# A two-layer trunk on one core: own weight buffers for the recurrence's gate branch and the first u projection, whose chunks go to single PSUM banks

## The chip, the cores and the metric

The kernel runs on one core of one Trainium2 chip. The metric is the device time of one execution in microseconds (us), the median of several runs. The engines are TensorE (PE, its weight loads PEld), VectorE (DVE), ScalarE (ACT), GpSimd (POOL) and SyncE (SP), which issues most DMAs.

## The reference: what is computed

Two layers over 1024 latent tokens with a prefix of 256 context tokens, width 1024. Only layer 0 matters here. Its input `h` (scaled and shifted by the adaLN modulation) is projected by `ab_w_in` to five branches of width 512:

```python
xl = depthwise_conv(p[..., :W], conv_w, conv_b)                 # branch x of the recurrence
...                                                             # gates r, i from xl; a, b; two scans
y_a = h_rec.astype(pp.dtype) * jax.nn.silu(pp[..., W:2 * W])    # gate branch
u = jax.nn.gelu(pp[..., 2 * W:3 * W])
v = jax.nn.gelu(pp[..., 3 * W:4 * W])
y_b = spatial_gating(u, v, sgu_ln_g, sgu_ln_b, sgu_w, sgu_b) * jax.nn.silu(pp[..., 4 * W:5 * W])
return jnp.concatenate([y_a, y_b], axis=-1) @ w_out
```

Layer 1 is a gated convolution beside differential attention. Modulation vectors (`silu(c) @ w_mod + b_mod`) for both layers are also computed.

## The kernel before, in words

Tokens lie on the free axis, 1280 of them in three chunks `CHUNKS` of 256, 512 and 512 (line 28). A projection gives 128 features at a time. Each float32 operand is split into a high part (rounded by a copy on ACT) and a low part (the difference, by default on POOL), and three products are added: hi x hi, lo x hi, hi x lo. With 8 steps of 128 along the input width that makes 24 matmuls for a chunk.

Weights for 128 features come by `wload` (line 143). It takes a raw tile (name `wraw`, two buffers), issues its DMA on SP, and splits it in two halves of four k-steps each: `whi` by ACT (line 138), `wlo` by POOL (line 141). `whi` and `wlo` have four buffers each in the pool `wp`, so two whole projections' worth, for all callers alike. A new `whi` has to wait until TensorE has used the old tile in its buffer for the last time.

A projection runs chunk by chunk over all k-steps (`proj3c_g`, line 167). So its first weight half is read for the last time in the middle of the last chunk, and its second half at the very end. `proj1_g` (line 180) has the same order for one chunk and any destination.

PSUM: `pj3` (line 260) gives tiles of three banks, two buffers, in turn to the projections `px`, `pg`, `pu`, `pz` and to the recurrence's gates `pgate`. `psb` (line 214) gives single banks of 512 columns, two buffers, to the modulation (`modp`, `modcp`, `gatep`) and to others later.

The recurrence handles four blocks of 128 features: `lru_x(f)` projects the x branch (conv follows on DVE), `lru_g(f)` the gate branch (line 396), `lru_rec(f)` makes four gates `pgate` by small matmuls and turns them to coefficients on ACT and DVE, `lru_scan(f)` scans. `mod_do` and `mod_c` (lines 475, 487) put a piece of modulation between them. Around the change TensorE's order is: `px` of block 3, `lru_rec(2)`, `lru_g(3)`, the first u projection `pu` (line 532, GELU per chunk into `ut0`), `lru_rec(3)`, then `pz` (weights `WZ0`) and the second `pu` (weights `WU1`).

TensorE's order is written by hand (line 55). The order of ACT, DVE, POOL and SP is set by a scheduler that simulates the program when it is built; each engine then works through its own list strictly in that order. In `lru_scan` (line 442) ACT takes a square root `tt` that needs DVE's product of line 433.

Of the kernel before, what the change touches and what calls it, by code (L numbers as in the profile page):

```python
# [11 lines left out]
F32R = mybir.dt.float32r  # L12
AF = mybir.ActivationFunctionType
# [29 lines left out]
def tile_hybrid_trunk(es: ExitStack, tc: tile.TileContext, A, out, scr=None):  # L43
    nc = tc.nc
    V, S, G, T, SY = nc.vector, nc.scalar, nc.gpsimd, nc.tensor, nc.sync

    def pool(name, space=None, **kw):
        if space is not None:
            kw["space"] = space
        return tc.tile_pool(name=name, bufs=1, reuse_waits="tile", **kw)  # L50
# [6 lines left out]
    wp = es.enter_context(pool("w"))  # L57
# [71 lines left out]
    def hs(c0, n):  # L129
        if c0 < CTX:  # L130
            return hhc[:, :, c0:c0 + n], hlc[:, :, c0:c0 + n]
        return hhl[:, :, c0 - CTX:c0 - CTX + n], hll[:, :, c0 - CTX:c0 - CTX + n]

    def split(hi, lo, src, he=None, le=None):
        he = he or S
        le = le or V
        if he is S:
            S.activation(hi, src, AF.Copy)  # L138
        else:
            he.tensor_copy(hi, src)  # L140
        le.tensor_tensor(lo, src, f32(hi), op=ALU.subtract)  # L141

    def wload(src, nk=8, le=None):
        raw = wp.tile([128, nk, 128], F32, name="wraw", tag="wraw", bufs=2)
        SY.dma_start(raw, src)
        res = []
        for h in range(nk // 4):
            hi = wp.tile([128, 4, 128], F32R, name="whi", tag="whi", bufs=4)
            lo = wp.tile([128, 4, 128], F32R, name="wlo", tag="wlo", bufs=4)
            split(hi, lo, raw[:, 4 * h:4 * h + 4], le=le or G)  # L150
            res.append((hi, lo))
        return res

    def run(gen):
        for _ in gen:
            pass
# [10 lines left out]
    def proj3c_g(ps, w):  # L167
        for c0, n in CHUNKS:
            o, (hh, hl_) = ps[:, 256 + c0:256 + c0 + n], hs(c0, n)
            for k in range(KT):  # L170
                hi, lo = w[k // 4]
                T.matmul(o, hi[:, k % 4], hh[:, k], start=k == 0, stop=False)  # L172
                T.matmul(o, hi[:, k % 4], hl_[:, k], start=False, stop=False)
                T.matmul(o, lo[:, k % 4], hh[:, k], start=False, stop=k == KT - 1)  # L174
                yield 0.68 * n / 512

    def proj3(ps, w):
        run(proj3c_g(ps, w))

    def proj1_g(o, w, c0, n):  # L180
        hh, hl_ = hs(c0, n)
        for k in range(KT):
            hi, lo = w[k // 4]
            T.matmul(o, hi[:, k % 4], hh[:, k], start=k == 0, stop=False)  # L184
            T.matmul(o, hi[:, k % 4], hl_[:, k], start=False, stop=False)  # L185
            T.matmul(o, lo[:, k % 4], hh[:, k], start=False, stop=k == KT - 1)  # L186
            yield 0.65 * n / 512

    def proj1(o, w, c0, n):
        run(proj1_g(o, w, c0, n))  # L190
# [23 lines left out]
    def psb(name="psb"):  # L214
        t = ps1.tile([128, 512], F32, name=name, tag="psb", bufs=2)
        return t
# [43 lines left out]
    def pj3(name):  # L260
        t = pj.tile([128, 1536], F32, name=name, tag="pj", bufs=2)
        return t
# [75 lines left out]
    for k in range(KT):  # L338
# [14 lines left out]
        if k + 1 < KT:  # L353
            hmod(k + 1, mb)
        next(gg)
    WX1 = wload(A["w_in0"][1], le=V)
    so_cm.__exit__(None, None, None)
    run(gx), run(gg)
# [7 lines left out]
    with pool("lrua") as lp, pool("lruc") as lc:  # L366
# [6 lines left out]
        def lru_x(f):  # L373
            if f:
                p = pj3("px")
                PROJ(proj3c_g(p, WX1 if f == 1 else wload(A["w_in0"][f])))
            else:
                p = px0
            xp = lp.tile([128, 1286], F32, name="xp", tag="xp", bufs=1)
            V.memset(xp[:, 0:2], 0.0)  # L380
            V.memset(xp[:, 258:260], 0.0)
            V.memset(xp[:, 1284:1286], 0.0)
            S.activation(xp[:, 2:258], p[:, 256:512], AF.Copy)
            for c0 in (512, 1024):
                S.activation(xp[:, c0 - 252:c0 + 260], p[:, c0:c0 + 512], AF.Copy)
            cw = P("convw")[:, 4 * f:4 * f + 4]
            xl = lt("xl", "xl", 2)
            V.tensor_scalar(xl, xp[:, 0:WC], cw[:, 0:1], P("convb")[:, f:f + 1], op0=ALU.mult, op1=ALU.add)
            for j in range(1, 4):
                V.scalar_tensor_tensor(xl, xp[:, j:j + WC], cw[:, j:j + 1], xl, op0=ALU.mult, op1=ALU.add)  # L390
            xh = lt("xh", "xh", 1, F32R)
            xo = lt("xo", "xo", 1, F32R)
            split(xh, xo, xl)
            XL[f] = (xl, xh, xo)

        def lru_g(f):
            if f:
                p = pj3("pg")
                PROJ(proj3c_g(p, wload(A["w_in0"][4 + f])))
            else:  # L400
                p = pg0
            sg = ld.tile([128, NTOK], F32, name="sg", tag="sg", bufs=2)
            S.activation(sg, p[:, 256:1536], AF.Tanh, scale=0.5)
            V.scalar_tensor_tensor(sg, sg, 1.0, p[:, 256:1536], op0=ALU.add, op1=ALU.mult)
            SG[f] = sg

        def lru_rec(f):
            (wh, wl), = wload(A["wg"][f], nk=4)
            mod_step()
            xl, xh, xo = XL[f]  # L410
            bs = []
            for d in range(2):
                i8 = 4 * d + f
                gts = []
                for g in range(2):
                    p = pj3("pgate")
                    m = 2 * d + g
                    for c0, n in ((0, 258), (258, 512), (770, 512)):
                        o = p[:, 254 + c0:254 + c0 + n]
                        T.matmul(o, wh[:, m], xh[:, c0:c0 + n], start=True, stop=False)  # L420
                        T.matmul(o, wh[:, m], xo[:, c0:c0 + n], start=False, stop=False)
                        T.matmul(o, wl[:, m], xh[:, c0:c0 + n], start=False, stop=True)
                    t = lt("gt", "gr" if g == 0 else "gx", 2)
                    S.activation(t, p[:, 254:1536], AF.Tanh, scale=0.5, bias=hb[:, 8 * g + i8:8 * g + i8 + 1])
                    gts.append(t)
                r, gi = gts
                tt = lt("tt", "tt", 2)
                S.activation(tt, r, AF.Tanh, scale=sp2[:, i8:i8 + 1], bias=sp2[:, i8:i8 + 1])
                S.activation(r, r, AF.Exp, scale=sn4[:, i8:i8 + 1], bias=sn4[:, i8:i8 + 1])
                V.scalar_tensor_tensor(gi, gi, 1.0, xl, op0=ALU.add, op1=ALU.mult)  # L430
                V.scalar_tensor_tensor(tt, r, 1.0, tt, op0=ALU.add, op1=ALU.mult)
                V.tensor_scalar(r, tt, -1.0, 1.0, op0=ALU.mult, op1=ALU.add)
                V.scalar_tensor_tensor(tt, r, 1.0, tt, op0=ALU.add, op1=ALU.mult)
                bs.append((r, gi, tt))
                mod_step()
            return bs
# [78 lines left out]
        PROJ = interleave  # L515
        mod_load()
        lru_x(0)
        lru_g(0)
        lru_x(1)
        lru_scan(0, lru_rec(0))  # L520
        lru_g(1)
        lru_x(2)
        lru_scan(1, lru_rec(1))
        lru_g(2)
        lru_x(3)
        lru_scan(2, lru_rec(2))
# [2 lines left out]
        u0 = u0_cm.__enter__()  # L529
        ut0 = u0.tile([128, NTOK], F32, name="ut0")  # L530
        zt0 = u0.tile([128, NTOK], F32, name="zt0")
        p = pj3("pu")
        proj3(p, wload(A["w_in0"][8]))
        for c0, n in CHUNKS:
            S.activation(ut0[:, c0:c0 + n], p[:, 256 + c0:256 + c0 + n], AF.Gelu_apprx_tanh)
        rec3 = lru_rec(3)
        while pend or late:
            mod_do()
# [11 lines left out]
    p = pj3("pz")  # L550
# [9 lines left out]
    with pool("sguw") as vw:  # L560
# [7 lines left out]
        p = pj3("pu")  # L568
# [48 lines left out]
        p = pj3("pz")  # L617
# [38 lines left out]
    for g in (2, 3):  # L656
        w = wload(A["w_in0"][8 + g])
# [5 lines left out]
        w = wload(A["w_in0"][12 + g])  # L663
# [110 lines left out]
    def pb(name):  # L774
        t = pbp.tile([128, 512], F32, name=name, tag="pb", bufs=2)
        return t
# [102 lines left out]
    for t in range(NT):  # L879
        p = pb("pv")  # L880
# [395 lines left out]
```

## Time and profile before

| | |
|---|---|
| median of three runs | 1142.79 us (1142.55 to 1142.98) |
| the profiled execution's own time | 1142.13 us |
| its span, first to last instruction | 1140.3 us |
| PE, PEld, DVE, ACT, POOL busy | 98%, 81%, 63%, 38%, 25% of the span |
| 72 to 205 us (the recurrence): PE busy | 130.07 of 133.00 us |
| 205 to 1130 us: PE busy | 921.16 of 925.00 us |

How to read it: a row of the timeline gives start, duration, engine, line, operation and tiles; brackets tell how long the engine was idle before, and what ended that. Matmuls are pipelined: a 512-column matmul is shown as 0.39 us long, but the next starts 0.23 us after it (0.12 us for 256 columns), so a stall of TensorE is a start-to-start distance above these. The program also ends 1.83 us later than its span says (1142.13 less 1140.3).

### The profile page before, as it was taken

How to read it: one execution, taken by the hardware profiler on the slowest of the kernel's cores; microseconds unless marked ns; L12 is line 12 of the kernel's file. 1: busy time of each engine (PE TensorE's matmuls, PEld its weight loads, DVE VectorE, ACT ScalarE, POOL GpSimd, SP SyncE). 2: the span in 40 equal slices, each digit the busy share in tenths (PEclk: the TensorE clock that was granted, in tenths of full speed). 3: DMA queues.
4: the chain of work that ended last, by engine and by line, in shares of the span. 5: the costliest groups of instructions: out<-in, count | busy, mean ns of one | idle time of the engine just before them, and what ended most of it. 6: DMA issues, size and time to landing. Idle time of an engine off the chain costs nothing.

```text
span 1140.3 us, 14964 instructions
## 1 busy us (share of the span) xinstructions
PE 1116.7 (98%) x5842; PEld 920.0 (81%) x5842; DVE 720.9 (63%) x1031; ACT 436.0 (38%) x687; POOL 284.6 (25%) x228
## 2 busy tenths in 40 slices
PE   6999999999999999999999999999999999999997
PEld 4777777888888888888788788888888888888886
DVE  6777986943412566537512876777676666738986
ACT  4463665620221243343212545444544444424210
POOL 0011112530240222258402322323421321220021
PEclk9999999999999999999999999999999999999999
DMA  9654542220241543336637243442531520127641
GB/s 368 258 178 157 185 154 105 94 97 1 86 142 54 180 152 116 120 130 208 230 93 190 91 112 78 111 118 65 143 96 40 144 91 20 48 73 240 203 148 74
DMA packets 78199, 148.08 MB, mean 130 GB/s; under 512 B 6305, under 2 KB 35873, under 8 KB 77233
## 3 DMA queue, kind: packets, MB, share of 16 engines
q1 hardware_dynamic: 71088, 128.25, 33.0%
q0 software_dynamic: 7040, 18.88, 7.3%
q8 instruction: 46, 0.75, 0.3%
q14 instruction: 25, 0.20, 0.1%
HBM read 112.49 MB, written 34.62 MB: 129 GB/s over the span
## 4 chain that ended last, share of the span: by engine, by line
PE 84%; DVE 5%; DMA 4%; issue 3%; ACT 3%; POOL 1%; SPq 0%; POOLq 0%; DVEq 0%; ACTq 0%
PE pout L683 5%; PE pout L685 5%; PE pout L684 5%; PE p L184 4%; PE p L185 4%; PE p L186 4%; PE psc L992 3%; PE pv L208 3%; PE pv L209 3%; PE pv L210 3%; PE psc L993 3%; PE atr L1015 3%; PE modp L221 2%; PE pz L172 2%; PE pz L174 2%
## 5 line engine op out<-in xcount | busy, mean ns | idle before, releaser
L141 POOL TENSOR_TENSOR wlo<-wraw,whi 128x512 fp32r<-128x512 f32 x86 | 134.3, 1565 | 427.8 <-ACT whi L138 415.6
L994 DVE TENSOR_REDUCE st<-psc 128x1 f32<-128x1280 f32 x64 | 95.1, 1486 | 39.5 <-PE psc L993 39.5
L683 PE MATMUL pout<-woh,yhi 128*128 128x512 f32 (+1 forms) x296 | 114.8, 388 | 0.3 <-DVE xres L1168 0.2
L685 PE MATMUL pout<-woh,ylo 128*128 128x512 f32 (+1 forms) x296 | 114.4, 386 | 0.0
L684 PE MATMUL pout<-wol,yhi 128*128 128x512 f32 (+1 forms) x296 | 114.1, 385 | 0.0
L996 ACT ACTIVATE e<-psc,st 128x1280 f32<-128x1280 f32 x64 | 85.2, 1331 | 71.7 <-DVE st L994 68.8
L184 PE MATMUL p<-hhl,whi 128*128 128x512 f32 x256 | 105.0, 410 | 0.0
L138 ACT ACTIVATE whi<-wraw 128x512 fp32r<-128x512 f32 x92 | 57.5, 628 | 122.8 <-PE p L185 27.2
L186 PE MATMUL p<-hhl,wlo 128*128 128x512 f32 x256 | 100.5, 393 | 0.0
L185 PE MATMUL p<-hll,whi 128*128 128x512 f32 x256 | 100.3, 392 | 0.0
L138 ACT ACTIVATE ah<-atr 128x512 fp32r<-128x512 f32 (+1 forms) x96 | 47.1, 525 | 64.6 <-PE atr L1015 64.2
L992 PE MATMUL psc<-k,qh 128*128 128x512 f32 (+1 forms) x192 | 67.1, 364 | 2.6 <-ACT e L996 2.5
L993 PE MATMUL psc<-k,ql 128*128 128x512 f32 (+1 forms) x192 | 68.7, 358 | 0.0
L683 PEld LDWEIGHTS pout<-woh,yhi 128*128 128x128 f32 x296 | 55.6, 188 | 12.4 <-issue 0.6
L685 PEld LDWEIGHTS pout<-woh,ylo 128*128 128x128 f32 x296 | 55.6, 188 | 11.6 <-DVE ylo L141 0.2
L684 PEld LDWEIGHTS pout<-wol,yhi 128*128 128x128 f32 x296 | 55.7, 188 | 11.3
L138 ACT ACTIVATE yhi<-yraw 128x512 fp32r<-128x512 f32 x36 | 22.5, 631 | 108.0 <-PE pout L684 72.3
L141 DVE TENSOR_TENSOR al<-atr,ah 128x512 fp32r<-128x512 f32 (+1 forms) x96 | 54.5, 594 | 6.3 <-ACT ah L138 6.2
L186 PEld LDWEIGHTS p<-hhl,wlo 128*128 128x128 f32 x256 | 48.0, 188 | 10.8
L185 PEld LDWEIGHTS p<-hll,whi 128*128 128x128 f32 x256 | 48.3, 189 | 8.2
L184 PEld LDWEIGHTS p<-hhl,whi 128*128 128x128 f32 x256 | 48.2, 188 | 8.0
L208 PE MATMUL pv<-wvh,hhl 128*128 128x512 f32 x128 | 52.0, 406 | 0.0
(325 smaller groups left out, 2815.8 us busy)
## 6 DMA issues: line engine op xcount, KB each, us to landing
wraw<-in_w_in_dram SPq DMA_DIRECT2D x42, 512.0 KB, 3.6
wm<-in_w_mod_dram SPq DMA_DIRECT2D x64, 256.0 KB, 4.7
wraw<-in_w_out_dram SPq DMA_DIRECT2D x16, 512.0 KB, 4.3
wm<-in_w_mod_dram SPq DMA_DIRECT2D x7, 1024.0 KB, 11.4
xt<-in_xcT_dram SPq DMA_DIRECT2D x8, 640.0 KB, 8.6
xres<-in_xc_dram SPq DMA_DIRECT2D x10, 512.0 KB, 4.0
wvr<-in_w_v_dram SPq DMA_DIRECT2D x8, 512.0 KB, 3.6
n_d<-xres SPq DMA_DIRECT2D x8, 512.0 KB, 2.6
```

Source lines behind the costliest of these rows:

```text
L138: S.activation(hi, src, AF.Copy)
L141: le.tensor_tensor(lo, src, f32(hi), op=ALU.subtract)
L184: T.matmul(o, hi[:, k % 4], hh[:, k], start=k == 0, stop=False)
L185: T.matmul(o, hi[:, k % 4], hl_[:, k], start=False, stop=False)
L186: T.matmul(o, lo[:, k % 4], hh[:, k], start=False, stop=k == KT - 1)
L208: T.matmul(p, hh[:, k], wh, start=k == 0, stop=False)
L683: T.matmul(o, hi[:, i], wh[:, c], start=first and i == 0, stop=False)
L684: T.matmul(o, hi[:, i], wl[:, c], start=False, stop=False)
L685: T.matmul(o, lo[:, i], wh[:, c], start=False, stop=not first and i == 3)
L992: T.matmul(o, qh[:, m, cu], KS[hd, m][:, c:c + n], start=True, stop=False)
L993: T.matmul(o, ql[:, m, cu], KS[hd, m][:, c:c + n], start=False, stop=True)
L994: V.tensor_reduce(st[:, m:m + 1], p[:, 256:1536], axis=AX.X, op=ALU.max, negate=True)
```

## The change

`wload` gets an optional pool `wq` for `whi` and `wlo`, with two buffers each there, one projection's worth. `lru_g(1)` to `lru_g(3)` and the first u projection use it with the recurrence's pool `lp`; `wraw` stays where it was. The first u projection no longer takes a three-bank tile: each of its chunks goes to a `psb` bank of its own.

```diff
-    def wload(src, nk=8, le=None):
+    def wload(src, nk=8, le=None, wq=None):
         raw = wp.tile([128, nk, 128], F32, name="wraw", tag="wraw", bufs=2)
         SY.dma_start(raw, src)
         res = []
         for h in range(nk // 4):
-            hi = wp.tile([128, 4, 128], F32R, name="whi", tag="whi", bufs=4)
-            lo = wp.tile([128, 4, 128], F32R, name="wlo", tag="wlo", bufs=4)
+            hi = (wq or wp).tile([128, 4, 128], F32R, name="whi", tag="whi", bufs=2 if wq else 4)
+            lo = (wq or wp).tile([128, 4, 128], F32R, name="wlo", tag="wlo", bufs=2 if wq else 4)
...
-                PROJ(proj3c_g(p, wload(A["w_in0"][4 + f])))
+                PROJ(proj3c_g(p, wload(A["w_in0"][4 + f], wq=lp)))
...
-        p = pj3("pu")
-        proj3(p, wload(A["w_in0"][8]))
+        w = wload(A["w_in0"][8], wq=lp)
         for c0, n in CHUNKS:
-            S.activation(ut0[:, c0:c0 + n], p[:, 256 + c0:256 + c0 + n], AF.Gelu_apprx_tanh)
+            p = psb("pu0")[:, 0:n]
+            proj1(p, w, c0, n)
+            S.activation(ut0[:, c0:c0 + n], p, AF.Gelu_apprx_tanh)
```

TensorE's list keeps its order, matmul for matmul. The lists of the other engines move in three places that matter below.

**Place 1.** ACT, from the middle of `lru_rec(2)` to the GELUs of the first `pu`. The numbers are those of the tiles: `wraw_1645` before and `wraw_1644` now hold the weights of the first `pu`; `wraw_1730` / `wraw_1732` the gate weights of `lru_rec(3)`; `wraw_1828` / `wraw_1830` are `WZ0`, `wraw_1838` / `wraw_1840` `WU1`; `pg_1517` is the projection of `lru_g(3)`. Before, first around `lru_rec(2)`:

```order
L429 ACTIVATE gt_1451<-gt_1451,sp_102 128x1282
L424 ACTIVATE gt_1482<-pgate_1472,hb_99 128x1282
L138 ACTIVATE whi_1651<-wraw_1645 128x512
L138 ACTIVATE xh_1395<-xl_1390 128x1282
L424 ACTIVATE gt_1494<-pgate_1484,hb_99 128x1282
```

and then, also before, around the end of `lru_g(3)`:

```order
L429 ACTIVATE gt_1482<-gt_1482,sp_102 128x1282
L138 ACTIVATE whi_1732<-wraw_1730 128x512
L442 ACT_TABLE_LOAD
L442 ACTIVATE tt_1496<-tt_1496 128x1282
L138 ACTIVATE whi_1830<-wraw_1828 128x512
L403 ACT_TABLE_LOAD
L403 ACTIVATE sg_1636<-pg_1517 128x1280
L138 ACTIVATE whi_1834<-wraw_1828 128x512
L138 ACTIVATE whi_1840<-wraw_1838 128x512
L535 ACT_TABLE_LOAD
```

Now, at the first of the two:

```order
L429 ACTIVATE gt_1451<-gt_1451,sp_102 128x1282
L424 ACTIVATE gt_1482<-pgate_1472,hb_99 128x1282
L138 ACTIVATE whi_1842<-wraw_1840 128x512
L138 ACTIVATE xh_1395<-xl_1390 128x1282
L424 ACTIVATE gt_1494<-pgate_1484,hb_99 128x1282
```

and at the second:

```order
L429 ACTIVATE gt_1482<-gt_1482,sp_102 128x1282
L138 ACTIVATE whi_1646<-wraw_1644 128x512
L442 ACT_TABLE_LOAD
L442 ACTIVATE tt_1496<-tt_1496 128x1282
L138 ACTIVATE whi_1650<-wraw_1644 128x512
L403 ACT_TABLE_LOAD
L403 ACTIVATE sg_1636<-pg_1517 128x1280
L536 ACT_TABLE_LOAD
```

The first `pu`'s two splits moved from `lru_rec(2)` and before it to the end of `lru_g(3)`, on either side of a square root, and took the places of the splits of `lru_rec(3)`'s and `WZ0`'s weights, which now stand further ahead. In the built program `whi_1646` waits for the last use of `lru_g(3)`'s first half, `whi_1650` for that of its second.

**Place 2.** SP's list from the load that follows `lru_g(3)`'s weights. Before:

```order
L145 DMA wraw<-in_w_in_dram 128x1024
L462 DMA ya_d<-gt 128x256
L462 DMA ya_d<-gt 128x1024
L145 DMA wraw<-in_wg_dram 128x512
L471 DMA wm<-in_w_mod_dram 128x512 x8
L145 DMA wraw<-in_w_in_dram 128x1024
```

Now:

```order
L145 DMA wraw<-in_wg_dram 128x512
L462 DMA ya_d<-gt 128x256
L145 DMA wraw<-in_w_in_dram 128x1024
L462 DMA ya_d<-gt 128x1024
L471 DMA wm<-in_w_mod_dram 128x512 x8
L145 DMA wraw<-in_w_in_dram 128x1024
```

The first `pu`'s raw weights now come earlier than all of this; the last load shown was `WZ0`'s and is now `WU1`'s, whose first split is the `whi_1842` of place 1.

**Place 3.** DVE's list near the end of the program, where the last output stage starts (`xres` is the residual, `pout` the output projection's PSUM bank). Before:

```order
L1144 TENSOR_TENSOR xres_9007<-xres_9007,rowln_g0_8740 128x1024
L1145 TENSOR_TENSOR xres_8928<-xres_8928,rowln_b0_8744 128x1024
L1144 TENSOR_TENSOR xres_9086<-xres_9086,rowln_g0_8740 128x1024
L1145 TENSOR_TENSOR xres_9007<-xres_9007,rowln_b0_8744 128x1024
L1144 TENSOR_TENSOR xres_9197<-xres_9197,rowln_g0_8740 128x1024
L1168 TENSOR_TENSOR xres_8802<-xres_8802,pout_8750 128x512
```

Now (lines are one higher there, tile numbers two higher):

```order
L1145 TENSOR_TENSOR xres_9009<-xres_9009,rowln_g0_8742 128x1024
L1146 TENSOR_TENSOR xres_8930<-xres_8930,rowln_b0_8746 128x1024
L1145 TENSOR_TENSOR xres_9088<-xres_9088,rowln_g0_8742 128x1024
L1169 TENSOR_TENSOR xres_8804<-xres_8804,pout_8752 128x512
L1146 TENSOR_TENSOR xres_9009<-xres_9009,rowln_b0_8746 128x1024
```

The first read of a `pout` bank moved ahead of two operations of 1024 columns.

## Rows read from the trace of the kernel before

**Rows 1.** The page: busy time and share of each engine.
```profile
PE 1116.7 (98%) x5842; PEld 920.0 (81%) x5842; DVE 720.9 (63%) x1031; ACT 436.0 (38%) x687; POOL 284.6 (25%) x228
```
**Rows 2.** Waits of PE: line, releaser, us in total, times, longest.
```profile
PE pgate L420 <- ACT gt L424: 0.9, 2, 0.6
...
PE pg L172 <- ACT gt L424: 0.5, 1, 0.5
```
**Rows 3.** Timeline of PE, first gate's last matmul and second gate's first, `lru_rec(3)`.
```profile
192.84 0.39 PE L422 MATMUL pgate<-xh,wlo 128*128 128x512 f32 x1
194.68 0.39 PE L420 MATMUL pgate<-xh,whi 128*128 128x258 f32 x1 [1.45 <-ACT ut L535]
```
**Rows 4.** Timeline of ACT, end of `lru_g(3)` and after.
```profile
174.86 0.63 ACT L138 ACTIVATE whi<-wraw 128x512 fp32r<-128x512 f32 x1 [4.10 <-issue]
...
178.59 1.28 ACT L442 ACTIVATE tt<-tt 128x1282 f32<-128x1282 f32 x1 [1.80 <-DVE tt L433]
179.77 0.61 ACT L138 ACTIVATE whi<-wraw 128x512 fp32r<-128x512 f32 x1
```
**Rows 5.** Timeline of PE, end of `lru_g(3)` and the first `pu`'s fifth k-step.
```profile
177.11 0.39 PE L173 MATMUL pg<-hll,whi 128*128 128x512 f32 x1
...
177.56 0.28 PE L172 MATMUL pu<-hhc,whi 128*128 128x256 f32 x1
...
178.99 0.28 PE L172 MATMUL pu<-hhc,whi 128*128 128x256 f32 x1
...
179.23 0.28 PE L174 MATMUL pu<-hhc,wlo 128*128 128x256 f32 x1
```
**Rows 6.** Timeline of POOL, the splits around 180 us.
```profile
175.57 1.55 POOL L141 TENSOR_TENSOR wlo<-wraw,whi 128x512 fp32r<-128x512 f32 x1 [12.03 <-DMA wm<-in_w_mod_dram]
180.47 2.08 POOL L141 TENSOR_TENSOR wlo<-wraw,whi 128x512 fp32r<-128x512 f32 x1 [3.34 <-ACT whi L138]
...
192.03 1.29 POOL L141 TENSOR_TENSOR wlo<-wraw,whi 128x512 fp32r<-128x512 f32 x1 [1.08 <-ACT whi L138]
```
**Rows 7.** Timeline of DVE, before and after ACT's square root.
```profile
170.79 1.50 DVE L431 SCALAR_TENSOR_TENSOR tt<-gt,tt 128x1282 f32<-128x1282 f32 x1 [0.54 <-ACT gt L429]
...
179.90 1.50 DVE L445 TENSOR_TENSOR gt<-gt,tt 128x1282 f32<-128x1282 f32 x1 [1.34 <-ACT tt L442]
```
**Rows 8.** Timelines of PE and DVE at the last output stage.
```profile
1071.38 0.39 PE L685 MATMUL pout<-woh,ylo 128*128 128x512 f32 x1
1072.02 0.47 PE L683 MATMUL pout<-woh,yhi 128*128 128x512 f32 x1 [0.24 <-DVE xres L1168]
...
1068.91 1.23 DVE L1145 TENSOR_TENSOR xres<-xres,rowln_b 128x1024 f32<-128x1024 f32 x1
1070.04 1.23 DVE L1144 TENSOR_TENSOR xres<-xres,rowln_g 128x1024 f32<-128x1024 f32 x1
```
**Rows 9.** Windows: us, busy of PE, PEld, DVE, ACT, POOL, PEclk, DMA share, GB/s.
```profile
159.00:160.00 1.00, 1.00 (x7) 0.86 (x6) 1.00 (x1) 1.00 (x2) 0.00 (x0) 1.00 0.34 129
160.00:161.00 1.00, 0.68 (x3) 0.20 (x2) 1.00 (x2) 1.00 (x1) 0.00 (x0) 1.00 0.01 4
```
**Rows 10.** Timeline of ACT: the split in `lru_rec(2)` and an exponential after it.
```profile
161.04 0.63 ACT L138 ACTIVATE whi<-wraw 128x512 fp32r<-128x512 f32 x1
...
169.30 1.46 ACT L429 ACTIVATE gt<-gt,sp 128x1282 f32<-128x1282 f32 x1
```
**Rows 11.** Windows after the last matmul, columns as in rows 9.
```profile
1132.40:1135.00 2.60, 0.05 (x1) 0.00 (x0) 2.41 (x5) 0.00 (x0) 1.00 (x1) 1.00 0.00 0
1135.40:1140.00 4.60, 0.00 (x0) 0.00 (x0) 1.42 (x2) 0.00 (x0) 0.05 (x1) 0.50 0.30 114
```
**Rows 12.** Timeline of PE at the start of the program.
```profile
11.63 1.31 PE L164 MATMUL px<-hhl,whi 128*128 128x512 f32 x2
12.74 0.42 PE L164 MATMUL px<-hlc,whi 128*128 128x256 f32 x1
...
15.36 1.23 PE L221 MATMUL modp<-wm,csil 128*32 128x256 f32 x16
```

## The prediction

> **What bounds the kernel now.** I read the busy shares first: TensorE (PE) works 98% of the span and no other engine more than 63% [rows 1]. So the time changes only by what adds or removes a stall of PE. The stretches by stage say the same: 130.07 of 133.00 us are busy in the recurrence and 921.16 of 925.00 us behind it, where a delay has no slack to be taken up in, so I carry every stall that comes or goes to the end, one for one. Then I read PE's waits for those within reach of the change. Three stand around the recurrence's third and last block: waits for ACT's sigmoids `gt` in `lru_rec(2)` (0.6 us the longest of two, and 0.5 us at the projection behind it) [rows 2], and the second gate of `lru_rec(3)`, which waits 1.45 us for the GELU that reads the first u projection `pu` [rows 3]. The first two are due to ACT's work on the gates, and the edit does not touch that. The third is what the edit aims at: the second gate wants the three-bank tile that `pu` holds. So the whole to be won near the change is under 3 us, and a new stall of 2 us decides the sign.
>
> **The gain at the gate.** With `pu` in single banks, the second gate of `lru_rec(3)` takes the three-bank tile of `lru_g(3)`, which DVE has read before PE comes to it. Before, the last matmul of the first gate starts at 192.84 and its follower at 194.68 [rows 3]; at 0.23 us from start to start it could have come at 193.07. Gain 194.68 - 193.07 = **1.61 us**. Nothing is late next: the gates behind wait for sigmoids of the gates before them, and the modulation's single banks, now shared with `pu`'s chunks, for GELUs that end before PE comes.
>
> **The gain at the tail.** At the last output stage PE starts a matmul 0.64 us after the one before it (1071.38 to 1072.02), because DVE reads a `pout` bank only after two operations of 1024 columns, 1.23 us each [rows 8]. In the new list that read stands ahead of one of them (place 3). Gain 0.64 - 0.23 = **0.41 us**; DVE's own work is the same, and its other 1024-column operation is not waited for by PE.
>
> **The loss at the first `pu`.** Here the change removes a cover. Before, `pu`'s weights had been split long before, into the common four buffers. Now they go to two buffers that `lru_g(3)`'s weights hold, and PE does the two projections back to back. The first half is no trouble: its buffer comes free in the middle of `lru_g(3)`'s last chunk, where ACT splits another tile at 174.86 now [rows 4] and POOL makes its low part from 175.57 to 177.12 [rows 6]; PE starts `pu` at 177.56 [rows 5]. The second half's buffer is free only when `lru_g(3)`'s last matmul has ended, at 177.11 + 0.39 = 177.50 [rows 5], and PE wants this half at `pu`'s fifth k-step, 1.5 us later: the high part at 178.99, the low part at 179.23 [rows 5].
>
> It can't be there. In ACT's new list its split stands behind the square root `tt`, which waits for DVE until 178.59, and a split in that very position ran from 179.77 to 180.38 [rows 4]. POOL then began the low part at 180.47 and took 2.08 us, to 182.55 [rows 6]. So PE's fifth step starts about 180.45 for 178.99, does two matmuls, and then stands until about 182.60 where it would have been at 179.23: **3.37 us** late, in two pieces of 1.46 and 1.91 us. What is queued behind the split on ACT (`sg`, the GELUs) only follows PE.
>
> POOL's 2.08 us is the one figure here to choose. Another split of the same size took 1.29 us [rows 6]; the slow one ran while DVE worked at 179.90 to 181.40 on two operands [rows 7], and DVE's place in time is unchanged, so I take 2.08 and keep 1.29 for the low end (a stall of 2.58).
>
> **A small loss ahead of it.** A split in `lru_rec(2)` on ACT, at 161.04 [rows 10], used the first `pu`'s weights, which had landed. Now the split in this place is that of `WU1`, and its load is put on SP right behind the eight modulation loads (place 2). The windows show these end at about 159.34 (a DMA share of 0.34 in the microsecond from 159) and almost nothing moving after 160 [rows 9]. The load is 128 x 1024 floats, 524 KB; at 129 GB/s over a share of 0.34, or 379 GB/s, it takes 1.38 us. An estimate from these rows is a landing from 160.72 (end 159.34) to 161.7 (end 160.3): 0 to 0.7 us of delay, and I take 0.3. Whatever it is, it goes on through the chain ACT exponential (169.30 to 170.76 [rows 10]), DVE 170.79 [rows 7], square root, split, low part, PE.
>
> The loads and splits of `lru_g(1)` and `lru_g(2)`, which also change buffers, and the loads of `lru_rec(3)`'s gates and `WZ0`, which now come earlier, I cost at nothing: the projection ahead of each is long past before they are wanted, and if that cover went, a split (0.61 us and 2.08 us) would be the price.
>
> **Sum.** +3.37 + 0.30 - 1.61 - 0.41 = **+1.65 us**. The profiled execution took 1142.13 us, so it would take 1143.8; it lies 0.66 us below the median of the runs, so the median becomes 1142.79 + 1.65 = **1144.4**. About 0.2% (2.3 us) is what a measurement of this kernel can tell from no change, so this most likely counts as the same. Bounds of this case: the low ends give 2.58 + 0 - 2.02 = +0.6 (1143.4), the high ones 3.37 + 0.7 - 1.61 without the tail's gain = +2.5 (1145.3).
>
> **The rivals.**
> - *The split comes in time (A).* If DVE's product for the square root came by 177.5, ACT would split at 177.55, and POOL, free since 177.12, would end at 178.18 + 1.29 = 179.5: a stall of 0.3. Then 0.3 + 0 to 0.3 - 2.02 = about -1.5, 1141.3; if ACT's earlier list also shortened the waits of 0.6 and 0.5 us [rows 2], -2.6, 1140.2. For it: ACT's list is otherwise in the old order, so nothing forbids 1 us; against it: the square root's wait for DVE of 1.80 us [rows 4] is the end of a chain that the change delays rather than hastens.
> - *`WU1`'s load lands late (B), slower.* ACT works its list in order, so a late load holds up the sigmoids and exponentials of `lru_rec(2)`, DVE, the square root and the second half's split. It decides from 0.64 us beyond the 0.3 taken, a landing at about 161.98: 1.65 + 0.64 = 2.29. At 162.6 the net is 1.65 + 1.26 = +2.9, 1145.7. For it: several loads are in flight just then; against it: the windows are all but empty after 160 [rows 9].
> - *TensorE falls to its lower clock (C), slower.* After the last matmul the granted clock is 1.00 (2.4 GHz) up to 1135.0 and 0.50 (1.2 GHz) from 1135.4 [rows 11]; before that fall PE did nothing. The stall idles PE too, but in two pieces. If it fell here, PE would work at half pace for a while. No row shows how long; the nearest is the start, where matmuls stand 1.11 us apart for two of 512 columns (0.46 later) and this lasts from 11.63 to 15.36 [rows 12]: half of 3.73 is 1.9 us more. Net +3.5, 1146.3. Against it: PE works between the pieces, and rows 11 still show full clock for more than 2 us after the last matmul.
>  The Trainium skill ("TensorE: Matmul & The Clock Gate", section "Why this matters for your kernels") advises against idle gaps between bursts of matmuls in the middle of a kernel, since the clock then goes back to half. By that rule the weight stall would cost more than its own length; rows 11 agree that idle time ends the full clock, and no row shows it for a gap as short as these.
> - *The change does not reach the end (D).* The gain and the loss may cancel, if POOL takes 1.29 us, the split goes a little earlier and the waits of `lru_rec(2)` shift: net 0, 1142.8.
>
> **Chances.** My forecast 0.53 (0.47 of it within 0.2%, 0.06 slower by more), A 0.13 (0.07 faster by over 0.2%, 0.06 within), B 0.16, C 0.10 (both slower), D 0.08 (within). Faster 0.07, same 0.47 + 0.06 + 0.08 = 0.61, slower 0.06 + 0.16 + 0.10 = 0.32. The range runs from A's first figure, a little lower, 1141.1, to just short of C, 1146.2; outside are A's larger gain and most of C, some 0.17.
>
> **What would show it.** Right: in the profile of the changed kernel no gate waits for `ut`; PE waits at the first `pu`'s fifth k-step, first for ACT's `whi`, then for POOL's `wlo`, some 3.4 us together; ACT's split follows the square root directly; and the tail's wait for `xres` is gone. The split of `WU1` shows whether ACT waits for its load near 161. Wrong: `whi` of the second half starting before 178 (A), a DMA as releaser of that split by a microsecond or more (B), a granted clock under 1.00 between 178 and 190 (C), or a stall in another place, of which the order gives no sign.

## The result and the profile after

| | before | after |
|---|---|---|
| median, us | 1142.82 (1142.55 to 1142.98, 4 runs) | 1151.1 (1149.37 to 1151.71, 4 runs) |
| ratio, 95% interval | | 1.007 (1.0058 to 1.0083) |
| profiled execution: span, us | 1140.3 | 1149.9 |

The change is slower by 8.3 us. The forecast was 1144.4 us and its range ended at 1146.2. The two profiled executions took 1142.13 and 1151.69 us, so what the traces explain below adds up to 9.6 us, 1.3 more than the medians differ by.

Busy time of each engine on the page of the changed kernel (before: [rows 1]), and its waits of TensorE (PE) for line, releaser, us in total, times, longest:

```profile
PE 1121.2 (98%) x5842; PEld 923.0 (80%) x5842; DVE 720.1 (63%) x1031; ACT 436.0 (38%) x687; POOL 288.0 (25%) x228
```
```profile
PE pout L684 <- DVE zt L647: 2.9, 1, 2.9
...
PE pu L184 <- ACT whi L138: 1.8, 1, 1.8
PE pu L186 <- POOL wlo L141: 1.8, 2, 1.6
...
PE pgate L420 <- ACT gt L424: 0.9, 2, 0.6
PE pg L172 <- ACT gt L424: 0.5, 1, 0.5
PE px L172 <- ACT xp L385: 0.4, 1, 0.4
```

The gate's wait for `ut` and the tail's for `xres` are gone; the wait for `zt` and that for `xp` are new. PE is also busy for 4.5 us more with the same 5842 matmuls, so they ran slower somewhere. As PE's order is unchanged, the start of one matmul in both traces tells where it went:

| PE starts | before | after | later by | added since |
|---|---|---|---|---|
| the start stage's last `pg` | 51.46 | 52.24 | 0.78 | 0.78 |
| the modulation in `lru_x(1)` | 62.93 | 64.46 | 1.53 | 0.75 |
| the first `pu` | 177.56 | 179.93 | 2.37 | 0.84 |
| the low part of its fifth k-step | 179.23 | 185.90 | 6.67 | **4.30** |
| the first gate of `lru_rec(3)` | 191.30 | 200.81 | 9.51 | **2.84** |
| its second gate | 194.68 | 202.56 | 7.88 | **-1.63** |
| the first `pout` | 365.84 | 376.60 | 10.76 | **2.88** |
| the last output stage (the matmul of [rows 8]) | 1072.02 | 1081.75 | 9.73 | -1.03 |
| the last matmul | 1132.17 | 1141.79 | 9.62 | -0.11 |

**The stall and the clock.** The timeline of PE in the changed kernel, at the first `pu`'s fifth k-step (before: [rows 5]), then the same stretch of the program as one window before, and windows in the changed kernel (us, busy of PE, PEld, DVE, ACT, POOL, then granted clock, DMA share, GB/s):

```profile
181.68 0.28 PE L186 MATMUL pu<-hhc,wlo 128*128 128x256 f32 x1
183.77 0.39 PE L184 MATMUL pu<-hhc,whi 128*128 128x256 f32 x1 [1.82 <-ACT whi L138]
183.99 0.28 PE L185 MATMUL pu<-hlc,whi 128*128 128x256 f32 x1
185.90 0.58 PE L186 MATMUL pu<-hhc,wlo 128*128 128x256 f32 x1 [1.63 <-POOL wlo L141]
```
```profile
178.00:190.00 12.00, 12.00 (x65) 10.36 (x64) 10.39 (x9) 4.95 (x5) 2.76 (x2) 1.00 0.16 56
```
```profile
183.00:184.00 1.00, 0.23 (x2) 0.23 (x2) 0.77 (x1) 0.98 (x3) 0.20 (x1) 1.00 0.00 0
184.00:185.00 1.00, 0.28 (x2) 0.07 (x1) 0.97 (x2) 1.00 (x1) 1.00 (x1) 0.74 0.00 0
185.00:186.00 1.00, 0.10 (x1) 0.10 (x1) 1.00 (x1) 0.99 (x2) 0.85 (x1) 0.50 0.00 0
186.00:191.00 5.00, 5.00 (x17) 4.42 (x18) 4.96 (x5) 1.94 (x3) 0.00 (x0) 0.50 0.32 108
191.00:192.00 1.00, 1.00 (x5) 0.77 (x5) 1.00 (x3) 0.00 (x0) 0.00 (x0) 0.85 0.00 0
```

The stall has the two pieces foretold. (A third wait, of 0.18 us, for the low part of the first half, where the prediction saw no trouble, costs nothing: PE only stands less long at the fifth step.) In the second piece the granted clock falls from 1.00 to 0.50, 2.4 to 1.2 GHz, and it comes back only after 191, though PE works without a gap from 186. The 2.84 us between the stall and the gate are this: the 18 matmuls from 185.90 to 191.48 take 5.58 us where before they took 3.0.

Behind the stall stand these rows of ACT and POOL (before: [rows 4, 6, 10]):

```profile
164.37 0.63 ACT L138 ACTIVATE whi<-wraw 128x512 fp32r<-128x512 f32 x1 [1.13 <-DMA wraw<-in_w_in_dram]
...
181.93 1.27 ACT L442 ACTIVATE tt<-tt 128x1282 f32<-128x1282 f32 x1 [2.84 <-DVE tt L433]
183.11 0.61 ACT L138 ACTIVATE whi<-wraw 128x512 fp32r<-128x512 f32 x1
```
```profile
183.80 2.05 POOL L141 TENSOR_TENSOR wlo<-wraw,whi 128x512 fp32r<-128x512 f32 x1 [3.34 <-ACT whi L138]
```

The split follows the square root, and POOL takes 2.05 us, as worked out. Every link (164.37, 181.93, 183.11, 183.80) is 3.33 or 3.34 us later than before, while PE comes to `pu` only 2.37 us later: the wait of 1.13 us for `WU1`'s load adds 0.97 us to the stall.

**The new wait at `pout`.** PE and DVE in the changed kernel:

```profile
373.36 0.39 PE L174 MATMUL pz<-hhl,wlo 128*128 128x512 f32 x1
376.60 0.50 PE L684 MATMUL pout<-woh,yhi 128*128 128x512 f32 x1 [2.85 <-DVE zt L647]
```
```profile
375.06 1.49 DVE L647 SCALAR_TENSOR_TENSOR zt<-zt,pz 128x1280 f32<-128x1280 f32 x1 [12.24 <-ACT zt L646]
```

Before, the first `pout` came 0.24 us behind the last `pz` and did not wait for DVE's reading of it, which began 1.5 us later:

```profile
365.60 0.40 PE L174 MATMUL pz<-hhl,wlo 128*128 128x512 f32 x1
365.84 0.39 PE L683 MATMUL pout<-woh,yhi 128*128 128x512 f32 x1
```
```profile
367.31 1.49 DVE L646 SCALAR_TENSOR_TENSOR zt<-zt,pz 128x1280 f32<-128x1280 f32 x1 [12.25 <-ACT zt L645]
```

In the changed kernel the first output projection waits until DVE has read the last `pz`. In the built programs the last `pz` lies in PSUM banks 5 to 7 before and in 2 to 4 now, and the first `pout` bank is bank 2 in both. The first `pu` took one three-bank tile; without it, every later tile from `lru_rec(3)` on lies in the other one of the two.

**The wait for `xp`.** ACT before, and then in the changed kernel, around 52 us:

```profile
51.08 0.63 ACT L138 ACTIVATE whi<-wraw 128x512 fp32r<-128x512 f32 x1 [1.41 <-PE px L164]
51.65 0.39 ACT L383 ACTIVATE xp<-px 128x256 f32<-128x256 f32 x1
51.94 1.08 ACT L385 ACTIVATE xp<-px 128x512 f32<-128x512 f32 x2
```
```profile
51.63 1.68 ACT L138 ACTIVATE whi<-wraw 128x512 fp32r<-128x512 f32 x3 [1.17 <-DMA wraw<-in_w_in_dram]
53.21 0.36 ACT L383 ACTIVATE xp<-px 128x256 f32<-128x256 f32 x1
53.48 1.07 ACT L385 ACTIVATE xp<-px 128x512 f32<-128x512 f32 x2
```

With their own buffers, splits that had to wait before are now ahead of the copies `xp`, behind a load; PE's next `px` needs those copies, and the step of the table behind it is 0.75 us longer. No run changes this order alone, but the step comes with the weight half: it is 0.60 to 0.75 us longer than before in the seven profiles that have it (the changed kernel's among them), and at most 0.06 us in the four others.

### The profile page after: what moved, and what is told of

Same layout as the page of the kernel before. It is cut to its first block, busy times and chain, and to the rows that moved or that the text cites. A ratio compares the mean times of both kernels' runs of the same rounds, so it can differ in the third digit from the quotient of the medians.

```text
span 1149.9 us, 14954 instructions
## 1 busy us (share of the span) xinstructions
PE 1121.2 (98%) x5842; PEld 923.0 (80%) x5842; DVE 720.1 (63%) x1031; ACT 436.0 (38%) x687; POOL 288.0 (25%) x228
## 4 chain that ended last, share of the span: by engine, by line
PE 88%; DVE 3%; ACT 2%; DMA 2%; issue 2%; POOL 1%; SPq 0%; POOLq 0%; DVEq 0%; ACTq 0%
PE pout L684 6%; PE pout L686 6%; PE pout L685 6%; PE p L184 5%; PE p L185 5%; PE p L186 5%; PE psc L993 3%; PE pv L208 3%; PE pv L209 3%; PE pv L210 3%; PE psc L994 3%; PE atr L1016 3%; PE modp L221 2%; PE pz L172 2%; PE pz L173 2%
## 5 line engine op out<-in xcount | busy, mean ns | idle before, releaser
L141 POOL TENSOR_TENSOR wlo<-wraw,whi 128x512 fp32r<-128x512 f32 x86 | 138.3, 1614 | 434.0 <-ACT whi L138 426.1
```

## Experiments

### The two halves apart

**The PSUM half alone** (`e1_psum`), against the changed kernel:

```diff
-                PROJ(proj3c_g(p, wload(A["w_in0"][4 + f], wq=lp)))
+                PROJ(proj3c_g(p, wload(A["w_in0"][4 + f])))
...
-        w = wload(A["w_in0"][8], wq=lp)
+        w = wload(A["w_in0"][8])
```

> Only the PSUM half of the change: the first u projection in single banks, its and lru_g's weights in the common four buffers. My theory: the 2.9 us wait of the first output projection matmul for DVE's zt comes from the PSUM half alone (the last pz now lies in the three banks that hold the first pout bank), so it is here too; no stall and no clock fall at the first pu, its and pg's matmuls 0.227 us apart, and no gate waits for ut (-1.6 us). Net about +0.3 us: 1143.1 us (1142 to 1144). Rival: the zt wait is a late echo of the weight stall; then it is gone here and the time is about 1140.8 us.

Measured: 1144.56 us, ratio 1.0017 (1.0008 to 1.0027). The wait for `zt` is there, 2.8 us; so it comes from the PSUM half alone and is no echo of the stall. No stall, and the gate comes 1.6 us earlier. The run costs 1.5 us more than expected, and the windows behind that wait show a cause (columns as above):

```profile
364.50:367.00 2.50, 0.10 (x1) 0.00 (x0) 1.09 (x1) 2.36 (x3) 0.00 (x0) 1.00 0.00 0
367.00:368.00 1.00, 0.55 (x2) 0.50 (x3) 0.97 (x2) 0.77 (x1) 0.00 (x0) 0.96 0.00 0
368.00:371.00 3.00, 3.00 (x8) 2.30 (x7) 3.00 (x3) 0.00 (x0) 0.00 (x0) 0.50 0.42 176
```

The clock fell here too, and not in this execution alone: over the whole span the ten runs have a mean granted clock of 0.995 to 0.997, those of the kernel before 0.998 to 0.999. In the changed kernel's profile it stayed at 1.00 behind an equally long wait:

```profile
374.00:376.50 2.50, 0.00 (x0) 0.00 (x0) 1.44 (x1) 2.50 (x3) 0.00 (x0) 1.00 0.00 0
376.50:379.00 2.50, 2.40 (x10) 1.99 (x11) 2.47 (x3) 0.42 (x1) 0.00 (x0) 1.00 0.05 20
```

**The weight half alone** (`e2_weights`): the buffers `wq=lp` stay, the first `pu` goes back to a three-bank tile.

```diff
-        w = wload(A["w_in0"][8], wq=lp)
         for c0, n in CHUNKS:
-            p = psb("pu0")[:, 0:n]
-            proj1(p, w, c0, n)
-            S.activation(ut0[:, c0:c0 + n], p, AF.Gelu_apprx_tanh)
+            S.activation(ut0[:, c0:c0 + n], p[:, 256 + c0:256 + c0 + n], AF.Gelu_apprx_tanh)
```

(with `p = pj3("pu")` and `proj3(p, wload(A["w_in0"][8], wq=lp))` ahead of the loop.)

> Only the weight half of the change: own two buffers for lru_g(1) to lru_g(3) and the first u projection, which goes back to a three-bank tile. My theory: stall of some 4 us at the fifth k-step of pu, granted clock 0.50 behind it for some 7 us (2.5 us lost), pg and pu matmuls 0.233 us apart, the gate's wait for ut small or gone because the stall has moved GELU and PE together, and no wait for zt at the first pout. About 1150 us (1148.5 to 1151.5). Rival: the zt wait is an echo of the stall; then it is here too and the time is 1152 to 1153 us.

Measured: 1148.58 us, ratio 1.0053 (1.0038 to 1.0068); stall, 0.50 behind it, no wait for `zt`. The gate's wait is gone here as well, without the PSUM half. ACT shows what it really was; before, and then in this run:

```profile
191.32 0.63 ACT L138 ACTIVATE whi<-wraw 128x512 fp32r<-128x512 f32 x1 [2.08 <-PE pu L173]
191.97 1.28 ACT L535 ACT_TABLE_LOAD   x1
193.27 1.36 ACT L535 ACTIVATE ut<-pu 128x256 f32<-128x256 f32 x3
```
```profile
185.41 1.28 ACT L535 ACT_TABLE_LOAD   x1
200.18 1.36 ACT L535 ACTIVATE ut<-pu 128x256 f32<-128x256 f32 x3 [13.49 <-PE pu L174]
```

Before, the GELU stood in ACT's list behind a split (`whi_1840`) that waits for the last use of `pu`'s own weights, and behind its table load: 1.95 us from 191.32 to 193.27. Either half alone takes that away: with the PSUM half the table load and two of the three GELUs stand ahead of that split, with the weight half that split is done long before. The gain at the gate is 1.6 us in each.

### The wait for `zt`

`e3_parity`, one added matmul of 128 columns into an unused three-bank tile; nothing else moves in any list, and in the built program the last `pz` is back in banks 5 to 7. The edit against the changed kernel:

```diff
             S.activation(ut0[:, c0:c0 + n], p, AF.Gelu_apprx_tanh)
+        T.matmul(pj3("skip")[:, 0:128], w[0][0][:, 0], hhl[:, 0, 0:128], start=True, stop=True)
         rec3 = lru_rec(3)
```

> The whole change, with one more 128-column matmul into an otherwise unused three-bank tile behind the first pu, so that the three-bank tiles alternate as they did before and the last pz lies away from the first pout bank. My theory: the 2.9 us wait for zt is gone, the rest stays: 2 to 3 us less than the changed kernel, about 1148.8 us. Rival (the wait is due to timing): no change, 1151 us.

Measured: 1148.99 us, ratio 1.0058 (1.0043 to 1.0073), and no wait for `zt`. So the wait is a matter of which banks, as expected.

### The clock

`e4_fill`: against `e3_parity`, fillers in the stall take the place of the one matmul. (DVE's list near the end of the program falls back to the old order of place 3, and a few entries of ACT's and SP's lists move far behind the stall.)

```diff
+                T.matmul(fp[:, 0:512], w[0][0][:, 0], hhl[:, 0, 0:512], start=True, stop=True)
...
+                    if k == 4:
+                        fill(8)
                     T.matmul(p, hi[:, k % 4], hh[:, k], start=k == 0, stop=False)
                     T.matmul(p, hi[:, k % 4], hl_[:, k], start=False, stop=False)
+                    if k == 4:
+                        fill(7)
```

> As the run with the extra tile, but with 15 filler matmuls of 512 columns (0.23 us each, results unused) where TensorE stands still for the first pu's second weight half: eight ahead of the fifth k-step and seven ahead of its low part. The stall itself stays as long. My theory: TensorE's idle time in the stall is what lowers the granted clock; with the fillers it stays 1.00 and the time is 2.5 us below that of the run with the extra tile, about 1146.3 us. Rival: the clock falls for another reason, or the fillers only add work: granted clock 0.50 as before, same time or up to 3.5 us more.

Measured: 1147.11 us, ratio 1.004 (1.0025 to 1.0055). Windows of `e3_parity`, then of `e4_fill`:

```profile
182.00:184.00 2.00, 0.51 (x2) 0.50 (x2) 1.05 (x1) 1.98 (x3) 0.48 (x1) 0.67 0.00 0
184.00:186.00 2.00, 0.67 (x3) 0.38 (x2) 1.97 (x2) 1.98 (x2) 1.57 (x1) 0.50 0.00 0
186.00:188.00 2.00, 2.00 (x11) 2.00 (x11) 1.96 (x2) 1.28 (x1) 0.00 (x0) 0.50 0.60 170
```
```profile
182.00:184.00 2.00, 2.00 (x11) 1.39 (x10) 0.95 (x1) 1.98 (x3) 0.39 (x1) 1.00 0.00 0
184.00:186.00 2.00, 1.99 (x10) 1.33 (x10) 1.97 (x2) 1.99 (x2) 1.68 (x1) 1.00 0.00 0
186.00:188.00 2.00, 2.00 (x15) 1.83 (x15) 1.96 (x2) 1.76 (x3) 0.00 (x0) 1.00 0.57 131
```

PE gets the weights no sooner: the fifth step's high part starts at 183.49 and 183.59 in the two, its low part at 185.62 and 185.74. The stall is a little shorter in the second, 4.18 us for 4.91, because PE comes to `pu` later there; but 3.63 us were enough for a fall in `e6_pad_change` below. Work that nobody needs keeps the clock up and makes the program 1.9 us faster, net of the tail's 0.4 us, which this run's order of DVE loses again. The mean granted clock is 0.998 to 0.999 in the four runs of `e4_fill` and 0.995 to 0.996 in those of `e3_parity`. So it is PE's standing still that lowers the clock here.

### The slower matmuls

In the changed kernel the 512-column matmuls of `lru_g(1)` to `lru_g(3)` and of the first `pu` start 0.233 us apart (179.70 to 179.93), before 0.227. My first theory was the addresses' place modulo 64 bytes.

`e5_pad_before` (the kernel before) and `e6_pad_change` (the changed one):

```diff
     hlc = hc.tile([128, KT, CTX], F32R, name="hlc")
+    hc.tile([128, 8], F32, name="padh")
```
```diff
                 p = pj3("pg")
+                if f == 1:
+                    lp.tile([128, 8], F32, name="pad")
```

> The kernel before, with 32 unused bytes per partition at the end of the pool of hhc and hlc; every engine's list is the same instruction for instruction, only addresses of tiles allocated on that side move by 32 bytes, among them hhc, hlc, the weights wvh and wvl of pv and the output weights woh and wol. My theory: a 512-column matmul starts 0.233 us after the one before it, and not 0.227, where the addresses of its two operands differ modulo 64 bytes. Before, that holds for 384 matmuls of pv and 240 of pout; with the pad for none of them. So pv goes from 0.233 to 0.227 us, and the time falls by 624 x 0.006 = 3.7 us, to 1139 us. Rival (the spacing comes from what other engines do, or from the tile): 1142.7 us, pv at 0.233.

> The changed kernel with 32 unused bytes in the recurrence's pool ahead of the new weight buffers; lists the same instruction for instruction. My theory as in the run with the pad before: pg and the first pu go from 0.233 to 0.227 us, 192 matmuls of 512 columns x 0.006 = 1.2 us less than the changed kernel, about 1149.9 us (its runs scatter by 1 us, so the distances in the trace decide). Stall, clock and the wait for zt as in the changed kernel. Rival (the spacing comes from POOL's and ACT's splits running beside): still 0.233.

Measured: 1142.95 us, ratio 1.0006 (0.9997 to 1.0015), and 1152.82 us, 1.0088 (1.0073 to 1.0103). `pg` stays at 0.233 us in the second, and `pv` goes only from 0.2326 to 0.2319 us in the first: the theory fell. (The second run's profile has a granted clock of 0.52 from 375 to 381, behind the wait for `zt`.)

`e9_low`, the same buffers in another place:

```diff
+    for tag in ("whi", "wlo"):
+        lb.tile([128, 4, 128], F32R, name=tag, tag=tag, bufs=2)
...
-                PROJ(proj3c_g(p, wload(A["w_in0"][4 + f], wq=lp)))
+                PROJ(proj3c_g(p, wload(A["w_in0"][4 + f], wq=lb)))
...
-        w = wload(A["w_in0"][8], wq=lp)
+        w = wload(A["w_in0"][8], wq=lb)
```

> The changed kernel, but the new weight buffers lie at the start of the recurrence's first pool, right behind hll (at 95.8 to 104 KB of a partition) and not at 173 to 181 KB; every engine's list is the same instruction for instruction. The theory of operands alike modulo 64 bytes fell with the two runs with pads. New theory: the distance of 0.233 us goes with weights that lie far from the moving operand (hhl and hll, 30 to 96 KB); then pg and the first pu go back to 0.227 us here, some 1.1 us less than the changed kernel. Rival: it goes with the tile being written and read in turn, or with POOL's splits; then 0.233 us stays.

Measured: 1150.31 us, ratio 1.0072 (1.0057 to 1.0087). The groups of `pg` from 85 to 178 us (count, busy us, mean ns of one), of before, of the changed kernel and of `e9_low`:

```profile
L174 PE MATMUL pg<-hhl,wlo 128*128 128x512 f32 x45 | 17.5, 390 | 0.0
```
```profile
L174 PE MATMUL pg<-hhl,wlo 128*128 128x512 f32 x45 | 17.8, 396 | 0.0
```
```profile
L174 PE MATMUL pg<-hhl,wlo 128*128 128x512 f32 x46 | 17.9, 390 | 0.0
```

Every list is the same, and of the operands of these matmuls only the weights lie elsewhere (other tiles of the recurrence move up by 8 KB with it). So the weights' place takes the 6 ns away. For 192 matmuls that is 1.2 us, of which 144 x 0.006 = 0.86 us lie ahead of `pu`, the table's 0.84. The medians, 1151.1 and 1150.31 us, lie too near each other to show it; the traces do.

### The shared buffers

`e10_own_u`: the first `pu` gets tags of its own, so two more buffers for each part.

```diff
-        w = wload(A["w_in0"][8], wq=lp)
+        w = wload(A["w_in0"][8], wq=lp, sx="u")
```

(`sx` is added to the tags of `whi` and `wlo`.)

> The changed kernel, with two more buffers of their own for the first u projection's weights in the recurrence's pool, so that they no longer wait for lru_g(3)'s; a few splits and multiplications move in the lists of ACT, DVE and SP with it. My theory: no stall at the fifth k-step of the first pu and no fall of the clock there (4.2 + 2.2 us less); distances of 0.233 us and the wait for zt stay. 1151.1 - 6.4 = about 1144.7 us. Rival: the stall comes from ACT's order alone (the square root ahead of the split), and stays at 3 us or more.

Measured: 1148.23 us, ratio 1.0042 (1.0026 to 1.0059). No stall and no fall of the clock at `pu`. But only 2.9 us come of the 6.4 hoped for. ACT's list, now other, makes PE wait for `gt` at `lru_g(2)`:

```profile
122.82 0.39 PE L172 MATMUL pg<-hhc,whi 128*128 128x256 f32 x1 [1.09 <-ACT gt L424]
```

DVE's list near the end has the old order, which loses the tail's 0.4 us. And in the profiled execution the clock falls behind the wait for `zt`, where it did not in the changed kernel's. That execution is the slowest of the four, 1149.29 us at a mean granted clock of 0.994; the fastest took 1146.07 us at 0.998.

### A version that beats both

`e7_psum_swap` is the PSUM half with the added matmul of `e3_parity`; `e8_best` adds the pad of `e5_pad_before` and one of 32 bytes ahead of the attention's tiles.

> Only the PSUM half, and the one extra matmul into an unused three-bank tile that lets the tiles alternate as before. My theory: the gate's gain of 1.4 to 1.6 us without the wait for zt, without stall and without a fall of the clock; 1142.7 - 1.5 = about 1141.2 us (1140.5 to 1142). Rival: the gate's gain is given back before the end, 1142.7 us.

> As the run of the PSUM half with the extra matmul, plus the 32 bytes at the end of the pool of hhc and hlc, plus 32 bytes ahead of the attention's q tiles, so that the 256 matmuls psc of 512 columns have both operands alike modulo 64 bytes as well. My theory: 1141.2 - 3.7 - 256 x 0.005 = about 1136.2 us. Rival (distances by other causes): 1141 us.

Measured: 1141.07 us, ratio 0.999 (0.998 to 0.9999), and 1140.53 us, ratio 0.9983 (0.9973 to 0.9992). So the PSUM half gains once the banks alternate as before, in the trace 1.6 us at the gate and 1.4 at the last matmul. The time of `e7_psum_swap` alone hardly shows it: its interval ends at 0.9999, and while six of its ten runs took 1140.0 to 1141.2 us, four took 1142.25 to 1142.88, as the kernel before does; why is open. All ten runs of `e8_best` took 1140.1 to 1140.8. The pads were put in for the theory that fell; that they add anything is not shown.

## Why the prediction was wrong, point by point

- **The gain at the gate**, 1.61 us: 1.63 measured. The mechanism was only half right: the tile mattered because the GELU stood behind a split and a table load, and the weight half alone removes that as well. So the right number was in part luck.
- **"Nothing is late next" is one of the two steps that put the time outside the range** (the other is the clock, below). I followed the three-bank tiles through `lru_rec(3)` and no further. One tile fewer swaps all later ones, and at the end of the stage the last `pz` lies under the first `pout`: 2.88 us, shown by `e1_psum` and `e3_parity`. The banks and the wait stand in the built program.
- **The loss at the first `pu`**, 3.37 us: right in place, order, pieces and releasers. With the next point's 0.97 it makes 4.34, for the table's 4.30.
- **The small loss ahead of it**, 0.3 us, at most 0.7: it was 0.97. The load landed 1.13 us after ACT wanted it (0.46 to 1.76 us in other runs with the weight half). Rival B decided from 0.94 in all, so it just came true beside the forecast.
- **The clock**, rival C with 0.10 and nothing in the sum: it came true. Its price of 1.9 us, taken from the program's start, measured 2.5 in the trace (2.84 less 48 x 0.006), and some 2.3 between `e3_parity` and `e4_fill` (1.9 and the tail's 0.4). I had set against it that PE works between the pieces; two matmuls there did not save the clock. The Trainium skill ("TensorE: Matmul & The Clock Gate", section "Why this matters for your kernels") warns of idle gaps in mid-kernel that bring the clock back to half; the trace agrees, with gaps of 1.82 and 1.63 us that are each shorter than those the page warns of, and there the measurement decides.
- **"The loads and splits of `lru_g(1)` ... I cost at nothing"** failed: splits of the weight half that may run earlier did so ahead of `xp`, 0.75 us.
- **No term for the weights' place**: 1.2 us.
- **The gain at the tail**, 0.41 us: PE's distance there is 0.22 us now, 0.42 gained. It goes with the order of DVE's list (place 3): the distance is 0.22 or 0.23 us in the six profiles that have the new order and 0.63 to 0.65 in the six that have the old one, `e7_psum_swap` and `e8_best` among these.

```profile
1081.53 0.39 PE L686 MATMUL pout<-woh,ylo 128*128 128x512 f32 x1
1081.75 0.39 PE L684 MATMUL pout<-woh,yhi 128*128 128x512 f32 x1
```

- **The cases were treated as alternatives.** Forecast, B and C are one chain: a later load makes the stall longer, and PE's standing still lowers the clock. They add up. Even the stall as foretold, 3.67 us with the small loss, would not have been safe: `e6_pad_change` lost its clock in one of 3.63.

Two entries of the table are most likely not the change's. The first 0.78 us: at that point the other runs stood 0.05 us earlier to 0.81 us later than before, without the weight half too (`e1_psum` 0.28, `e7_psum_swap` 0.53). And of the 1.03 us gained ahead of the last output stage only 0.42 are the tail's; `e5_pad_before`, whose lists are those of the kernel before, comes 0.90 us nearer over the same stretch.

The runs of the changed kernel lie 2.3 us apart, and no run shows why. Further falls of the clock are not it: all four have a mean granted clock of 0.996. Elsewhere falls do come in some executions only, and the mean shows them: `e6_pad_change` took 1154.02 and 1153.21 us at 0.992, 1152.42 and 1151.03 us at 0.996.

## What to carry to other kernels

Where a tile leaves a pool that alternates between two buffers, look up where every later tile of that pool now lies, and what the next pool puts on top of it: the built program tells. "Own buffers" for two adjacent projections are own only if each has its own; otherwise the second one's split waits for the first one's last matmul. And price a stall of TensorE with the clock behind it, as an addition and not as a rival.

## What the runs showed of the hardware that I had not expected

- Two idle times, of 1.57 to 1.82 and 1.33 to 1.63 us, with two matmuls between took the clock to 0.50 in each of the five profiles that had them, and in the changed kernel's 5 us of dense work passed at 0.50 before it rose (186 to 191). One idle time of 2.85 us took it down in `e1_psum`, `e6_pad_change` and `e10_own_u`, and not in the changed kernel or `e9_low`. What decides it there stays open.
- 512-column matmuls whose weights lie at 173 to 181 KB of a partition, with their moving operand at 30 to 96 KB, start 0.233 us apart; with weights at 14 to 30 or at 96 to 104 KB it is 0.227. The place modulo 64 bytes is not the reason. Which property of the place it is was not tried. The kernel before has such a difference too: the 512-column matmuls of `pv`, with moving operands at 147 to 200 KB, start 0.234 us apart on average where the weights `hhl` and `hll` lie at 30 to 96 KB, and 0.229 where `hhc` and `hlc` lie at 213 to 229 KB. That fits operands far apart; but `psc`, with operands 3 to 31 KB apart, is at 0.231 to 0.234, so distance alone does not explain it.
